# RG-LRU gate products one column tile later, two attention gate tiles moved behind them, and the rotary key's low part on GpSimd, in a two-layer decoder trunk

## The chip, the cores and the metric

The kernel runs on one core of a Trainium2 chip. The time is in microseconds (us) of device time for one execution of the whole program, both layers. The engines are TensorE (PE in the profile, PEld for its weight loads), VectorE (DVE), ScalarE (ACT), GpSimd (POOL) and SyncE (SP), which issues the DMAs. All five run at once, each through its own instructions in a fixed order, and wait for each other on semaphores.

## The reference

A trunk of two layers on x of 1024 tokens and 1024 features, float32. In each layer one combined projection of the normalised input feeds three token mixers; each branch is multiplied by a SiLU gate of the same projection, and the branches go through one output projection into the residual:

```python
h = rmsnorm(x, norm_gain)
proj = h @ w_in
(gq, gk, gv, gb, ga, gz, mq, mkv, mkr, mz, lx, lz) = jnp.split(proj, offsets, axis=-1)
# A: gated DeltaNet (GDN), 4 heads of 128, chunks of 64
o_a = rmsnorm(gated_delta_rule(q, k, v, g, beta), gdn_out_norm) * jax.nn.silu(gz)
# B: latent attention, 8 heads; mkr is the rotary key shared by all heads
k_pe = apply_rope(mkr[:, :, None, :], cos, sin)
o_b = causal_block_attention(qf, kf, vm) * jax.nn.silu(mz)
# C: RG-LRU, 512 channels in 8 blocks of 64
u = causal_dwconv(lx, lru_conv_w) + lru_conv_b
r = jax.nn.sigmoid(u @ w_r + b_r)          # block-diagonal
i = jax.nn.sigmoid(u @ w_i + b_i)
log_a = -8.0 * r * jax.nn.softplus(-a_param)
a = jnp.exp(log_a)
b = jnp.sqrt(-jnp.expm1(2.0 * log_a)) * (i * u)
o_c = associative_scan(h_t = a_t * h_(t-1) + b_t) * jax.nn.silu(lz)
return x + jnp.concatenate([o_a, o_b, o_c], axis=-1) @ w_out
```

## The kernel before

Activations stand with features on the 128 partitions and the 1024 tokens along the free axis. **Products in three passes.** Every float32 operand of a matmul is split into a high part (a copy rounded to the format TensorE takes) and a low remainder, and `mm3` adds high x high, low x high and high x low, so three matmuls per product. `split` makes the two parts of an activation (ACT copies, DVE or POOL subtracts), `load_w` those of a weight: DMA to `wst`, `whi` by a DVE cast (by ACT for the small gate weights), `wlo` by a POOL subtraction.

**Column tiles.** `in_tile` makes one tile of the combined projection, 128 columns by 1024 tokens: 8 input blocks x 2 halves x 3 passes = 48 matmuls into a PSUM tile `pbig`. There are two such PSUM tiles, so a tile can begin only when the tile two before it has been read out; the weight buffers are two deep as well. After a tile stands what reads it: `conv` (one ACT pass and three DVE passes) for a convolved column tile, or a SiLU (`silu2`: ACT tanh, one DVE pass `z`) in `gate_tile`, whose result goes to memory (`mzd` for the attention gates mz, `gzd` for the GDN gates gz).

**What sets the order.** The program is traced in one order, and a scheduler then places instructions on their engines by priority, in the order in which their inputs can be ready. The matmuls of `in_tile` are traced inside a region whose priority is lowered by 20000: they are filler that goes wherever other work leaves TensorE free; the conversions and convolutions beside them are raised by as much. Two consecutive matmuls of a tile may so have other work between them.

**The stages of a layer.** `phase_a` runs GDN for two pairs of heads. While one pair goes through its steps (tokens, `pre`, the inverse of the chunk matrices on DVE in 30 small steps, `prep`, `scan`, and a normalisation with gating, whose last passes are `gzh` on DVE), a generator yields filler tiles; `FILL` says how many at which step. The fillers of pair 0 are gz0, gz1, some mz tiles and the q, k, v tiles of pair 1; those of pair 1 are the latent tiles of the attention, gz2, gz3 and the other mz tiles. There are 8 mz tiles: `MZ1` of them go with pair 1, `MZ2` after the RG-LRU, and the rest, 8 - MZ1 - MZ2, with pair 0. Then comes `lru`: four lx tiles with convolution and gate products; for all four then exponent, square root and scan; four lz tiles with the gating (`of`, split into `oh`, `ol`); the late mz tiles; and the loads of GDN's output (`oaf`, split into `oah`, `oal`). `out_proj` with w_o1 follows: 16 half tiles of 24 matmuls each over `oa` and `oh`, into the banks `pspr`, which DVE adds to the residual `xt`. Meanwhile `split_latents` prepares the attention, among it the rotary key (`rope`, then `kp` and `kl`). Phase C is the attention, with the rest of the output projection in it.

In `lru` the u tiles (`lu`, four of them) lie in buffers of a pool that opens when GDN's pool closes; `uh` and `ul` have one buffer each. The gate products of one tile are 12 matmuls into the two banks `pssc`: two gates x two halves x three passes.

## Time and profile before

| | us |
|---|---|
| median of three runs | 2173.77 (2172.88 to 2176.52) |
| the profiled execution | 2180.79 |
| its span, first to last instruction | 2179.0 |
| TensorE busy | 2060.8 (95%), 10380 matmuls |
| VectorE busy | 1320.7 (61%) |
| ScalarE busy | 882.8 (41%) |
| GpSimd busy | 731.1 (34%) |
| mean granted TensorE clock | 0.986 |

A row of the timeline gives the start in us from the beginning of the span, the duration, the engine, the line of the kernel, the operation, output<-input with shapes, and in brackets how long the engine stood idle before it and what it waited for. In layer 0 the RG-LRU runs from about 495 to 610 us and the first output projection from there to about 700; in layer 1 they begin at about 1570 and 1670 us. A matmul of 512 columns is shown 0.39 us long, but the next starts 0.227 us after it: the end is modelled.

### The profile page before, as it was taken

The numbers are of one execution on the slowest core, as the hardware profiler recorded it, in microseconds if no ns is written. First come the engines' busy times: TensorE is split into PE (matmuls) and PEld (weight loads), VectorE is DVE, ScalarE is ACT, GpSimd is POOL, SyncE is SP. The second block draws the span as 40 slices with busy tenths as digits, with TensorE's granted clock in tenths as the row PEclk, the third lists the DMA queues.
The fourth block names the chain that finished last, engine by engine and source line by source line (L and its number), as shares of the span: only waits on it lengthen the run. The fifth ranks groups of instructions, "written<-read, shape, count | busy, mean of one in ns | idle before, by whom it ended". The sixth has DMA issues, their size and how long they took to land. (4 is left out here: it accounts for less than half of the span.)

```text
span 2179.0 us, 28798 instructions
## 1 busy us (share of the span) xinstructions
PE 2060.8 (95%) x10380; PEld 1683.7 (77%) x10380; DVE 1320.7 (61%) x2498; ACT 882.8 (41%) x1790; POOL 731.1 (34%) x784
## 2 busy tenths in 40 slices
PE   6999999999989999999889999999998999999997
PEld 3788887787767788888668888788876877878874
DVE  6546556555852777776665476474468237676766
ACT  5251244135720554553542413531375125444534
POOL 3222333234452333332242313333336323232322
PEclk9999999999999999999999999999999999999999
DMA  4223212323253115335421331134223520335172
GB/s 142 80 79 97 78 58 93 95 80 102 67 176 131 31 38 185 103 122 181 144 82 49 93 102 46 62 107 131 69 68 113 172 96 27 114 108 170 60 232 97
DMA packets 135102, 222.07 MB, mean 102 GB/s; under 512 B 37808, under 2 KB 60336, under 8 KB 134960
## 3 DMA queue, kind: packets, MB, share of 16 engines
q1 hardware_dynamic: 134960, 220.24, 31.1%
q8 instruction: 82, 1.34, 0.3%
q14 instruction: 60, 0.49, 0.1%
HBM read 147.31 MB, written 72.88 MB: 101 GB/s over the span
## 5 line engine op out<-in xcount | busy, mean ns | idle before, releaser
L112 POOL TENSOR_TENSOR wlo<-wst,whi 128x1024 fp32r<-128x1024 f32 (+3 forms) x196 | 316.1, 1613 | 834.5 <-DVE whi L111 308.9
L121 PE MATMUL pbig<-h,whi 128*128 128x512 f32 x1216 | 484.4, 399 | 8.9 <-ACT h L127 5.9
L123 PE MATMUL pbig<-h,wlo 128*128 128x512 f32 x1216 | 485.1, 399 | 4.0 <-POOL wlo L112 4.0
L122 PE MATMUL pbig<-h,whi 128*128 128x512 f32 x1216 | 484.7, 399 | 3.4 <-DVE h L128 1.6
L121 PEld LDWEIGHTS pbig<-h,whi 128*128 128x128 f32 x1216 | 231.3, 190 | 55.1 <-ACT h L127 6.7
L122 PEld LDWEIGHTS pbig<-h,whi 128*128 128x128 f32 x1216 | 230.8, 190 | 52.4 <-POOL h L128 4.5
L123 PEld LDWEIGHTS pbig<-h,wlo 128*128 128x128 f32 x1216 | 231.0, 190 | 48.5 <-POOL wlo L112 5.3
L86 ACT ACTIVATE P<-pS,mx,scq 128x512 f32<-128x512 f32 (+1 forms) x192 | 128.2, 671 | 155.2 <-DVE mx L89 84.2
L111 DVE CAST whi<-wst 128x1024 fp32r<-128x1024 f32 x92 | 78.2, 850 | 154.7 <-PE pbig L122 122.5
L95 POOL TENSOR_SCALAR P<-P,mx 128x128 f32<-128x128 f32 (+6 forms) x112 | 81.2, 725 | 217.3 <-DVE mx L773 130.1
L109 ACT CAST whi<-wst 128x256 fp32r<-128x256 f32 (+2 forms) x104 | 46.2, 446 | 203.3 <-DMA wst<-in_w_uq 106.2
L127 ACT CAST pth<-pstp 128x512 fp32r<-128x512 f32 x192 | 91.2, 479 | 76.0 <-PE pstp L802 76.0
L762 DVE TENSOR_REDUCE mx<-pS 128x1 f32<-128x512 f32 (+1 forms) x192 | 106.4, 554 | 17.1 <-PE pS L756 11.1
L128 DVE TENSOR_TENSOR ptl<-pstp,pth 128x512 fp32r<-128x512 f32 x192 | 104.7, 551 | 14.7 <-ACT pth L127 13.9
L86 ACT ACT_TABLE_LOAD x81 | 103.9, 1283 | 2.7 <-PEq L1176 0.7
L802 PE MATMUL pstp<-con,P 128*128 128x128 f32 x576 | 97.8, 275 | 5.7 <-DVE P L777 5.0
L92 DVE TENSOR_TENSOR xt<-pspj,xt 128x512 f32<-128x512 f32 x96 | 66.2, 689 | 53.4 <-PE pspj L123 24.6
L121 PE MATMUL pspj<-lh,whi 128*128 128x512 f32 x208 | 85.5, 411 | 6.7 <-DVE k L128 6.0
L802 PEld LDWEIGHTS pstp<-con,P 128*128 128x128 f32 x576 | 71.7, 141 | 25.2 <-DVE P L777 7.3
L813 PE MATMUL pspo<-pth,vh 128*128 128x512 f32 x192 | 79.0, 412 | 6.6 <-ACT pth L127 6.6
L123 PE MATMUL pspj<-lh,wlo 128*128 128x512 f32 x208 | 82.7, 398 | 0.4 <-POOL wlo L112 0.4
L122 PE MATMUL pspj<-ll,whi 128*128 128x512 f32 x208 | 83.0, 399 | 0.0
(270 smaller groups left out, 4566.1 us busy)
## 6 DMA issues: line engine op xcount, KB each, us to landing
wst<-in_w_in SPq DMA_DIRECT2D x76, 512.0 KB, 3.6
x<-xt SPq DMA_DIRECT2D x128, 256.0 KB, 3.4
xt<-x SPq DMA_DIRECT2D x112, 256.0 KB, 3.5
mzd<-z SPq DMA_DIRECT2D x16, 512.0 KB, 3.5
wst<-in_w_o SPq DMA_DIRECT2D x16, 512.0 KB, 3.6
mz<-mzd SPq DMA_DIRECT2D x32, 256.0 KB, 2.9
wst<-in_w_o SPq DMA_DIRECT2D x64, 128.0 KB, 2.1
xk<-x SPq DMA_DIRECT2D x32, 256.0 KB, 4.2
```

The lines of the kernel that those rows point to most:

```text
L86: self.nc.scalar.activation(out, in_, func, **kw)
L95: self.nc.gpsimd.tensor_scalar(out, a, s, 1.0, ALU.mult, ALU.mult)
L111: nc.vector.tensor_copy(hi[:, :n], st[:, :n])
L112: (eng or nc.gpsimd).tensor_tensor(lo[:, :n], st[:, :n], hi[:, :n].bitcast(F32), ALU.subtract)
L121: nc.tensor.matmul(out, ah, bh, start=(j == 0), stop=False)
L122: nc.tensor.matmul(out, ah, bl, start=False, stop=False)
L123: nc.tensor.matmul(out, al, bh, start=False, stop=(j == n - 1))
L127: self.nc.scalar.copy(hi, x)
L128: (eng or self.nc.vector).tensor_tensor(lo, x, hi.bitcast(F32), ALU.subtract)
L762: nc.vector.tensor_reduce(mx[:, j : j + 1], S[j], AX.X, ALU.max, negate=True)
L802: nc.tensor.transpose(tp[:, qi * 128 : qi * 128 + 128], P[qi][:, kb * 128 : kb * 128 + 128], self.ident)
L813: nc.tensor.matmul(po[:, w], vh[:, vs], th[:, w], start=(j == 0), stop=False)
```

## The change

Three things. First, the gate products of tile m are a generator now: its first part (split of u, the gate's weight) is traced behind lx tile m, its second part (the products) behind lx tile m+1. The first matmul of each tile's gates is also pinned, in the order of TensorE's instructions, behind every one traced before it. Second, one filler mz tile fewer is made in each GDN pair (MZ1 from 4 to 3, MZ2 from 0 to 2), and these two are made in `lru`: one before the gate products of tile 3, the other behind the lz tiles. Third, the subtraction that gives `kl`, 64x512 twice per layer, moves from DVE to GpSimd.

```diff
--- before.py
+++ after.py
@@ -113,12 +113,14 @@
         return (hi[:, :n].rearrange("p (k c) -> p k c", k=nk),
                 lo[:, :n].rearrange("p (k c) -> p k c", k=nk))
 
-    def mm3(self, out, pairs):
+    def mm3(self, out, pairs, behind=False):
 
         nc = self.nc
         n = len(pairs)
         for j, (ah, al, bh, bl) in enumerate(pairs):
-            nc.tensor.matmul(out, ah, bh, start=(j == 0), stop=False)
+            first = nc.tensor.matmul(out, ah, bh, start=(j == 0), stop=False)
+            if behind and j == 0:
+                self.tc.keep_in_program_order(first)
             nc.tensor.matmul(out, ah, bl, start=False, stop=False)
             nc.tensor.matmul(out, al, bh, start=False, stop=(j == n - 1))
 
@@ -524,17 +526,16 @@
     def lru(self, l):
         nc, pa, par = self.nc, self.pa, self.par
         st, res = [], []
-        for m in range(4):
-            p = self.in_tile(l, MT_LX + m)
-            u = pa.tile([128, T], F32, name="u", tag="lu", bufs=4)
-            with self.prio(-self.LOW):
-                self.conv(u, p, par[:, C_LCONV + 4 * m : C_LCONV + 4 * m + 4], bias=par[:, C_LCB + m : C_LCB + m + 1])
+
+        def gate_products(m, u):
+
             uh = pa.tile([128, T], F32R, name="uh", tag="uh", bufs=1)
             ul = pa.tile([128, T], F32R, name="ul", tag="ul", bufs=1)
             for n, eng in ((0, nc.gpsimd), (1, nc.vector)):
                 s = slice(n * H2, (n + 1) * H2)
                 self.split(uh[:, s], ul[:, s], u[:, s], eng)
             hi, lo = self.load_w(self.i["w_lru"][l, m], 2, 128, pool=pa)
+            yield
             gt = []
             for k in range(2):
                 t = pa.tile([128, T], F32, name="lg", tag=("lr", "li")[k], bufs=4)
@@ -542,7 +543,7 @@
                 for n in range(2):
                     s = slice(n * H2, (n + 1) * H2)
                     pg = self.bank("sc")
-                    self.mm3(pg, [(hi[:, k], lo[:, k], uh[:, s], ul[:, s])])
+                    self.mm3(pg, [(hi[:, k], lo[:, k], uh[:, s], ul[:, s])], behind=(k == 0 and n == 0))
                     self.act(t[:, s], pg, AF.Sigmoid, bias=par[:, cb : cb + 1])
                 gt.append(t)
             r, ii = gt
@@ -551,6 +552,26 @@
             th = ii
             self.act(th, r, AF.Tanh, scale=self.c8[:, m : m + 1])
             st.append((u, r, th))
+
+        late = iter(range(8 - self.MZ2, 8))
+
+        def late_gate():
+            for h in itertools.islice(late, 1):
+                self.gate_tile(l, MT_MZ + h, self.mzd[h], pa.tile([128, T], F32, name="z", tag="lt", bufs=2))
+
+        prev = None
+        for m in range(4):
+            p = self.in_tile(l, MT_LX + m)
+            u = pa.tile([128, T], F32, name="u", tag="lu", bufs=4)
+            with self.prio(-self.LOW):
+                self.conv(u, p, par[:, C_LCONV + 4 * m : C_LCONV + 4 * m + 4], bias=par[:, C_LCB + m : C_LCB + m + 1])
+            for _ in prev or ():
+                pass
+            prev = gate_products(m, u)
+            next(prev)
+        late_gate()
+        for _ in prev:
+            pass
         for m in range(4):
             u, a, th = st[m]
             self.act(a, a, AF.Exp, scale=self.c8n[:, m : m + 1])
@@ -577,8 +598,7 @@
                         self.silu2(z[:, s], p[:, s])
                 self.gate_split(st[m][2][:, s], 0.5, z[:, s], oh[:, s], ol[:, s], nc.vector if m == 3 else nc.gpsimd)
             res.append((oh, ol))
-        for h in range(8 - self.MZ2, 8):
-            self.gate_tile(l, MT_MZ + h, self.mzd[h], pa.tile([128, T], F32, name="z", tag="lt", bufs=2))
+        late_gate()
         oa = []
         for h in range(4):
             f = pa.tile([128, T], F32, name="oaf", tag="li", bufs=4)
@@ -655,7 +675,7 @@
             kr = self.rope(kx[0:64, s], 64, s)
             nc.scalar.copy(kp[0:64, s], kr)
             nc.scalar.copy(kp[64:128, s], kr)
-            self.tt(kl[0:64, s], kr, kp[0:64, s].bitcast(F32), ALU.subtract)
+            nc.gpsimd.tensor_tensor(kl[0:64, s], kr, kp[0:64, s].bitcast(F32), ALU.subtract)
 
             nc.scalar.copy(kl[64:128, s], kl[0:64, s].bitcast(F32))
         self.kp, self.kl = kp, kl
@@ -1002,8 +1022,8 @@
             self.gdn_norm(pr, Q)
             go(99)
 
-    MZ1 = 4
-    MZ2 = 0
+    MZ1 = 3
+    MZ2 = 2
     FILL = ((1, 1, 2, 0, 1), (1, 0, 3, 0, 2))
 
     LAG = 0.1
```

What this does to the instruction order, at three places of layer 0 (layer 1 has the same shapes). Names in it: u, uh, ul are the RG-LRU's convolved tile and its two parts, gzh GDN's gating, pbig a column tile's PSUM, h the normalised input; a number tells buffers apart.

The handover from GDN to RG-LRU, on DVE, before:

```order
L111 CAST whi_4146<-wst_4144 128x1024
L89 SCALAR_TENSOR_TENSOR gzh_3939<-pspr_3934,onh_346,gzh_3939 128x512
L944 TENSOR_SCALAR onh_9697<-par_9291 128x1
L89 SCALAR_TENSOR_TENSOR u_4007<-pbig_3958,par_185,u_4007 128x1023
L89 SCALAR_TENSOR_TENSOR u_4007<-pbig_3958,par_185,u_4007 128x1022
L89 SCALAR_TENSOR_TENSOR u_4007<-pbig_3958,par_185,u_4007 128x1021
L111 CAST whi_4242<-wst_4240 128x1024
L128 TENSOR_TENSOR ul_4013<-u_4007,uh_4012 128x512
L89 SCALAR_TENSOR_TENSOR u_4103<-pbig_4054,par_185,u_4103 128x1023
```

and now:

```order
L111 CAST whi_4100<-wst_4098 128x1024
L89 SCALAR_TENSOR_TENSOR gzh_3821<-pspr_3816,onh_346,gzh_3821 128x512
L964 TENSOR_SCALAR onh_9697<-par_9291 128x1
L89 SCALAR_TENSOR_TENSOR u_3889<-pbig_3840,par_185,u_3889 128x1023
L89 SCALAR_TENSOR_TENSOR u_3961<-pbig_3912,par_185,u_3961 128x1023
L89 SCALAR_TENSOR_TENSOR u_3889<-pbig_3840,par_185,u_3889 128x1022
L89 SCALAR_TENSOR_TENSOR u_3961<-pbig_3912,par_185,u_3961 128x1022
L89 SCALAR_TENSOR_TENSOR u_3889<-pbig_3840,par_185,u_3889 128x1021
L89 SCALAR_TENSOR_TENSOR u_3961<-pbig_3912,par_185,u_3961 128x1021
L130 TENSOR_TENSOR ul_3895<-u_3889,uh_3894 128x512
L92 TENSOR_TENSOR u_3889<-u_3889,lg_3977 128x1024
```

Before, the three passes of tile 0's convolution stood together and those of tile 1 behind the low part of tile 0; now the passes of the two tiles alternate, and the low part of tile 0 stands behind all six. The cast ahead of the last gzh is that of lx tile 3 now, and was that of lx tile 2.

The same place on TensorE, before: the end of lx tile 1 and the gate products of tile 0, 47 matmuls behind the end of lx tile 0 (L122 and L123 are the second and third pass of a product):

```order
L123 MATMUL pbig_4054<-h_107,wlo_4051 128x512
L121 MATMUL pbig_4054<-h_108,whi_4050 128x512
L122 MATMUL pbig_4054<-h_116,whi_4050 128x512
L121 MATMUL pssc_4025<-uh_4012,whi_4020 128x512
L123 MATMUL pbig_4054<-h_108,wlo_4051 128x512
L122 MATMUL pssc_4025<-ul_4013,whi_4020 128x512
L123 MATMUL pssc_4025<-uh_4012,wlo_4021 128x512
L121 MATMUL pssc_4030<-uh_4012,whi_4020 128x512
L121 MATMUL pbig_4150<-h_101,whi_4146 128x512
```

and now, from the last two matmuls of lx tile 1 on (L124 and L125 are the second and third pass now):

```order
L124 MATMUL pbig_3912<-h_116,whi_3908 128x512
L125 MATMUL pbig_3912<-h_108,wlo_3909 128x512
L121 MATMUL pbig_4008<-h_101,whi_4004 128x512
L121 MATMUL pssc_3967<-uh_3894,whi_3902 128x512
L124 MATMUL pssc_3967<-ul_3895,whi_3902 128x512
L125 MATMUL pssc_3967<-uh_3894,wlo_3903 128x512
L121 MATMUL pssc_3972<-uh_3894,whi_3902 128x512
L124 MATMUL pbig_4008<-h_109,whi_4004 128x512
```

Before, the gate products of tile 0 stood at the end of lx tile 1; now they stand behind the first matmul of lx tile 2. The gate products of tile 1 stand behind the end of lx tile 2, and so on.

The end of the inverse of pair 1, on DVE (inv and itmp are its steps, z a gate's pass), before:

```order
L92 TENSOR_TENSOR itmp_2731<-inv_2730 64x58
L92 TENSOR_TENSOR inv_2730<-inv_2730,itmp_2731 64x2x29
L92 TENSOR_TENSOR itmp_2731<-inv_2730 64x30
L92 TENSOR_TENSOR inv_2730<-inv_2730,itmp_2731 64x30
L393 COPY inv_2730<-inv_2730 64x32x32
L111 CAST whi_3473<-wst_3471 128x1024
L89 SCALAR_TENSOR_TENSOR z_3304<-z_3304,pbig_3255 128x1024
```

and now:

```order
L92 TENSOR_TENSOR inv_2671<-inv_2671,itmp_2672 64x5x26
L92 TENSOR_TENSOR itmp_2672<-inv_2671 64x108
L89 SCALAR_TENSOR_TENSOR z_3245<-z_3245,pbig_3196 128x1024
L92 TENSOR_TENSOR inv_2671<-inv_2671,itmp_2672 64x4x27
L92 TENSOR_TENSOR itmp_2672<-inv_2671 64x84
L92 TENSOR_TENSOR inv_2671<-inv_2671,itmp_2672 64x3x28
L92 TENSOR_TENSOR itmp_2672<-inv_2671 64x58
L92 TENSOR_TENSOR inv_2671<-inv_2671,itmp_2672 64x2x29
L92 TENSOR_TENSOR itmp_2672<-inv_2671 64x30
L92 TENSOR_TENSOR inv_2671<-inv_2671,itmp_2672 64x30
L395 COPY inv_2671<-inv_2671 64x32x32
L111 CAST whi_3577<-wst_3575 128x1024
```

The z pass that stood behind the copy at the end of the steps now stands seven steps ahead of that end.

The end of the RG-LRU on GpSimd, before (ol and oal are the low parts of the RG-LRU's and of GDN's output, wlo is lz tile 3's weight):

```order
L112 TENSOR_TENSOR wlo_4571<-wst_4568,whi_4570 128x1024
L128 TENSOR_TENSOR ol_4421<-of_4428,oh_4420 128x512
L128 TENSOR_TENSOR oal_4641<-oaf_4638,oah_4640 128x1024
L128 TENSOR_TENSOR ol_4489<-of_4492,oh_4488 128x512
L128 TENSOR_TENSOR ol_4489<-of_4496,oh_4488 128x512
L128 TENSOR_TENSOR oal_4647<-oaf_4644,oah_4646 128x1024
L112 TENSOR_TENSOR wlo_4665<-wst_4662,whi_4664 128x1024
```

and now:

```order
L112 TENSOR_TENSOR wlo_4512<-wst_4509,whi_4511 128x1024
L130 TENSOR_TENSOR oal_4641<-oaf_4638,oah_4640 128x1024
L130 TENSOR_TENSOR ol_4430<-of_4433,oh_4429 128x512
L130 TENSOR_TENSOR ol_4430<-of_4437,oh_4429 128x512
L130 TENSOR_TENSOR oal_4647<-oaf_4644,oah_4646 128x1024
L130 TENSOR_TENSOR oal_4653<-oaf_4650,oah_4652 128x1024
L112 TENSOR_TENSOR wlo_4583<-wst_4580,whi_4582 128x1024
L130 TENSOR_TENSOR oal_4659<-oaf_4656,oah_4658 128x1024
L130 TENSOR_TENSOR ol_4498<-of_4501,oh_4497 128x512
```

The first wlo of the rows of now is again lz tile 3's; the second, the weight of the second late mz tile, has come in between the third and the fourth oal.

## The prediction

> **What bounds the kernel now.** I read the page first, then the windows around the RG-LRU stage, then TensorE's waits there, then the timeline of the engines that it waits for.
>
> ```profile
> span 2179.0 us, 28798 instructions
> PE 2060.8 (95%) x10380; PEld 1683.7 (77%) x10380; DVE 1320.7 (61%) x2498; ACT 882.8 (41%) x1790; POOL 731.1 (34%) x784
> ```
>
> TensorE is busy for 95% of the span, and the change neither adds nor removes a matmul. So the time can move in two ways only: by what TensorE stands still (2179.0 − 2060.8 = 118 us), and by what it does at the lower clock. The windows (columns: PE, PEld, DVE, ACT, POOL busy, granted clock, DMA share, GB/s) show where layer 0 has such time:
>
> ```profile
> 470.00:520.00 50.00, 49.80 (x252) 39.20 (x251) 22.77 (x47) 17.10 (x38) 17.11 (x22) 1.00 0.32 106
> 560.00:570.00 10.00, 7.59 (x26) 5.50 (x25) 5.48 (x4) 9.20 (x10) 4.05 (x2) 0.83 0.15 52
> 605.00:610.00 5.00, 4.63 (x12) 3.34 (x12) 4.42 (x5) 2.95 (x5) 5.00 (x4) 0.66 0.01 4
> 648.00:655.00 7.00, 6.60 (x22) 5.30 (x23) 0.94 (x2) 0.00 (x0) 2.26 (x1) 0.76 0.57 185
> 1684.00:1688.00 4.00, 4.00 (x12) 3.08 (x11) 2.35 (x4) 0.62 (x1) 0.00 (x0) 0.56 0.89 323
> ```
>
> Where GDN hands over to RG-LRU (470 to 520), TensorE loses nothing: 49.80 of 50 us at clock 1.00. It loses in the gate products (560 to 570) and at the head of the output projection. The list of all of TensorE's waits (us in total, times, longest) has seven rows that fall wholly in these two places of the two layers:
>
> ```profile
> PE pssc L122 <- POOL ul L128: 5.9, 6, 1.6
> PE pssc L121 <- ACT uh L127: 2.6, 2, 1.8
> PE pspr L121 <- DVE xt L92: 4.6, 2, 3.7
> PE pspr L121 <- ACT oh L127: 3.9, 1, 3.9
> PE pspr L122 <- DVE ol L128: 3.0, 2, 1.6
> PE pspr L122 <- POOL oal L128: 2.5, 2, 1.8
> PE pspr L123 <- POOL wlo L112: 1.3, 1, 1.3
> ```
>
> Gate products (the first two rows) 8.5 us, output projection 15.3: together 23.8 us in 16 waits. These the change can reach.
>
> **What it saves.** *Gate products.* Before a gate product stand a convolution (ACT 1.21, three DVE passes 3.9), the half's copy and its remainder:
>
> ```profile
> 506.10 1.21 ACT L86 ACTIVATE u<-pbig,par 128x1024 f32<-128x1024 f32 x1 [11.72 <-PE pbig L123]
> 507.39 3.91 DVE L89 SCALAR_TENSOR_TENSOR u<-pbig,par,u 128x1023 f32<-128x1023 f32 x3
> 513.29 1.13 ACT L127 CAST uh<-u 128x512 fp32r<-128x512 f32 x2
> 514.15 1.30 POOL L128 TENSOR_TENSOR ul<-u,uh 128x512 fp32r<-128x512 f32 x1
> ```
>
> That is 1.2 + 3.9 + 0.6 + 1.3 = 7 us. In the changed order the gates of tiles 1, 2 and 3 stand 39 to 43 filler matmuls behind the tile's end, at 0.227 us each 9 to 10 us and more with the other gates between: the 8.5 us of waits go. *Output projection.* One whole tile (48 matmuls, 10.9 us) more now stands between the last gates and w_o1; the waits there for oh, ol, oal and wlo (3.9 + 3.0 + 2.5 + 1.3 = 10.7) are each shorter than this and go. *Rotary key.* The two waits for xt, 3.7 and 0.9, stand here:
>
> ```profile
> 644.52 1.25 POOL L673 TENSOR_TENSOR rw<-rw 64x512 f32<-64x512 f32 x1
> 646.46 0.68 DVE L92 TENSOR_TENSOR kl<-rw,kp 64x512 fp32r<-64x512 f32 x1 [3.17 <-ACT kp L656]
> 647.67 1.27 DVE L92 TENSOR_TENSOR xt<-pspr,xt 128x512 f32<-128x512 f32 x2
> ```
>
> DVE stood 3.17 us in front of kl, and the xt that frees TensorE's bank stood behind it. With kl on GpSimd, DVE is past it, so 4.6 us go. GpSimd now stands there instead. What is behind it is the next wlo, which it would begin about 1.3 us later than now (a 64x512 operation of GpSimd took 1.25 there); the matmuls of that weight come 24 matmuls, 5.5 us, later, so I cost this at nothing (0 to 1.5 us).
>
> To the 23.8 us add 16 × 0.16 = 2.6, since a matmul is shown 0.39 long but the next may start 0.227 after it, so each wait costs 0.16 more than its idle time. And the clock:
>
> ```profile
> 562.77 0.50 PE L121 MATMUL pssc<-uh,whi 128*128 128x512 f32 x1 [1.79 <-ACT uh L127]
> 564.13 0.50 PE L122 MATMUL pssc<-ul,whi 128*128 128x512 f32 x1 [0.62 <-POOL ul L128]
> ...
> 566.96 0.63 PE L121 MATMUL pbig<-h,whi 128*128 128x512 f32 x1
> 567.38 0.63 PE L122 MATMUL pbig<-h,whi 128*128 128x512 f32 x1
> ```
>
> After these waits matmuls start 0.42 us apart instead of 0.227 for some 3.4 us; 8 of them lose 1.6 us. Four of the windows above show this (clock 0.83, 0.66, 0.76, 0.56), all behind waits that go: 4 × 1.6 = 6.3. Saved in all: 23.8 + 2.6 + 6.3 = **32.7 us**.
>
> The Trainium skill ("TensorE: Matmul & The Clock Gate", Part 1) says the array falls to half rate only after an idle window of about 3.4 us. Here it fell after waits of 1.79 and 0.62 us, so the trace goes further than the rule. By the rule only the waits of 3.7 and 3.9 us would have cost clock, the saving would be 2 × 1.6 = 3.2 us less, and the forecast 2180 us.
>
> **What it costs.** *The handover.* In the changed order tiles lx0 and lx1 are both finished when GDN's normalisation ends, since u's buffers open only then, and DVE has both convolutions to do at once. It alternates them: u0, u1, u0, u1, u0, u1. They stand behind the gzh pass of the last quarter, and that behind a weight cast that waits for lx1's last matmuls. TensorE's next matmul, the first of lx2, needs u0's bank. The same pieces in the profile of before:
>
> ```profile
> 505.67 0.39 PE L123 MATMUL pbig<-h,wlo 128*128 128x512 f32 x1
> 505.94 0.69 DVE L111 CAST whi<-wst 128x1024 fp32r<-128x1024 f32 x1 [1.35 <-PE pbig L122]
> 506.55 0.74 DVE L89 SCALAR_TENSOR_TENSOR gzh<-pspr,onh,gzh 128x512 f32<-128x512 f32 x1
> ```
>
> From the last matmul of the tile (505.67, call it T) to DVE's first convolution pass (507.39) it is 1.7 us. Now u0's third pass is the fifth of the row: T + 1.7 + 5 × 1.30 = T + 8.2. Only then lx2's first matmul runs, and right behind it stand gates 0, which before had lx1's 47 matmuls in front of them: the copy uh0 (0.6) to T + 8.8, then ul0 on GpSimd (1.3 to 1.8) to T + 10.3. TensorE runs two matmuls in that time; it loses 10.3 − 0.2 − 0.5 + about 0.2 for the second half = 9.8 us. The lower end is 8 us (uh0 and ul0 found ready sooner), the upper 12 (ul 1.87 and DVE's half beside it 1.76). The lower clock behind it: 1.6. The transposes before it:
>
> ```profile
> 495.71 5.60 POOL L95 TENSOR_SCALAR at<-at,ms 128x128 f32<-128x128 f32 x16 [1.85 <-DVE ms L92]
> 499.21 1.08 PE L501 MATMUL pspr<-con,at 128*128 128x128 f32 x4
> ```
>
> have 18 filler matmuls in front of them instead of 33, 3.4 us less cover, and GpSimd gives out four scaled blocks per 1.4 us where TensorE takes 1.08. The chain ahead is shorter too, as no gate tile lies in it; I put 1.0 (0 to 3). Sum 9.8 + 1.6 + 1.0 = **12.4 us a layer** (9 to 16), where nothing is lost now.
>
> *The inverse of pair 1.* TensorE arrives there one tile earlier, because one filler tile has gone from each pair; it needs the bank of gz2, whose gating pass now stands inside the long chain of inverse steps on DVE. Now it stands behind the chain:
>
> ```profile
> 374.53 0.69 DVE L111 CAST whi<-wst 128x1024 fp32r<-128x1024 f32 x1 [3.97 <-PE pbig L122]
> 375.62 2.33 DVE L92 TENSOR_TENSOR itmp<-inv 64x84 f32<-64x84 f32 x1
> 403.52 0.24 DVE L92 TENSOR_TENSOR itmp<-inv 64x84 f32<-64x84 f32 x1
> 404.77 0.18 DVE L92 TENSOR_TENSOR inv<-inv,itmp 64x30 f32<-64x30 f32 x1
> 408.01 0.50 PE L121 MATMUL pbig<-h,whi 128*128 128x512 f32 x1 [0.66 <-DVE z L89]
> 409.39 0.50 PE L123 MATMUL pbig<-h,wlo 128*128 128x512 f32 x1 [0.64 <-POOL wlo L112]
> ```
>
> The chain ends at 404.95 and loses the 3.97 us wait for the cast; it also loses one GpSimd operation beside it (each makes two steps last 2.33 instead of 0.24, so 4.2). The pass stands seven steps, 1.7 us, ahead of its end: about 404.95 − 4.0 − 4.2 − 1.7 + 1.2 (its own length) = 396 to 398. TensorE arrives at 394 to 396. I take 3.0 us (0 to 5), and 0.8 for an even chance of the lower clock, less the 1.6 that the two waits above cost now: **2.2 a layer**.
>
> *The last late tile.* Its wlo stands on GpSimd behind two oal, which wait for an oaf load, which waits for DVE's of:
>
> ```profile
> 591.68 1.06 ACT L127 CAST oah<-oaf 128x1024 fp32r<-128x1024 f32 x1 [2.46 <-DMA oaf<-oad]
> 592.82 3.47 POOL L128 TENSOR_TENSOR oal<-oaf,oah 128x1024 fp32r<-128x1024 f32 x1 [0.86 <-ACT oah L127]
> 597.07 2.40 POOL L112 TENSOR_TENSOR wlo<-wst,whi 128x1024 fp32r<-128x1024 f32 x1 [0.78 <-PE pbig L123]
> ```
>
> Two oal (2.85 to 3.5 each) and the wlo (2.4) are 8 to 9.4 us between the load and the third matmul of a tile that covers 10.9; the load itself came 2.46 us late. I take 2.5 us (0 to 5), and 0.7 (0 to 1.5) for lz3, whose bank waits for lz1's pass: **3.2 a layer**.
>
> **Sum.** 2 × (12.4 + 2.2 + 3.2) = 35.6 lost, 32.7 saved: +2.9 us. The profiled run took 2180.79 us, 1.8 more than its span and 7.0 more than the median of the runs; it becomes 2183.7, and the median 2173.77 becomes **2177**. About 0.2%, 4.3 us, is what a measurement of this kernel can tell from no change. By the ends of the handover alone the sum goes from −4 to +10.
>
> **Rivals.** *Only the handover pays* (25%). The inverse chain is short enough and GpSimd early enough that both later stalls are nothing; the waits of 2 × 1.6 on the inverse go too. Then −32.7 + 24.8 − 3.2 = −11: 2163. For it: both prices have 0 as their lower end. Against: two more tiles stand on GpSimd's queue at the place where it is already fullest (605:610 has it busy 5.00 of 5).
>
> *GpSimd becomes the bound at the end of RG-LRU* (23%). If the oaf load lands more than about 2 us later than TensorE's start of lz3, the late tile's wlo costs its upper 5 us plus 1.6 of clock, and the oal behind it come late to w_o1, so that 1.8 + 0.7 us stay: (5 + 1.6 − 2.5) × 2 + 2.5 = +11 over my sum, 2188. For it: oal took 3.47 and 2.85 us there, of 128x1024, when DVE worked beside it. Against: the tile's own 10.9 us.
>
> *Gates and projection go on waiting* (4%). The pinned first product could leave TensorE's order as it was; then the gate waits (8.5) stay and so does the handover without a stall: 2173.8 − 4.6 for xt = 2169, on the edge of what can be told. Against: the instruction order shows the gates moved.
>
> **Chances.** Forecast 48% (half of it within 0.2%, two fifths slower, one tenth faster), the rivals 25% faster, 23% slower and 4% same. Faster 0.25 + 0.05 = 0.30, same 0.24 + 0.04 = 0.28, slower 0.23 + 0.19 = 0.42. The range takes the first rival's 2163 and the second's 2188: 2163 to 2189; the forecast's own is 2170 to 2184.
>
> **What would show it.** Right: in each layer a wait of 7 to 8.5 us before lx2's first matmul, released by DVE's u, then one of 1 to 2 us for ul; DVE's row of six alternating convolution passes right before; no wait for uh or ul of later gates; none of over 1 us for xt in the first output projection. Wrong: less than 5 us lost there, or more than 8 us in waits for wlo and oal between the gates and w_o1. I would be most wrong if the handover's loss were hidden after all, since it is three quarters of what I charge.

## The result, and the profile after: 2.7% slower

The changed kernel takes 2232.87 us (median of 4 runs, 2231.05 to 2235.77), the kernel before, on the same chip, 2175.14 (2172.88 to 2180.05): a ratio of 1.0268, 95% interval 1.0250 to 1.0286. It is slower, by 58 us, where 3 us were forecast; the time lies far above the range, which ended at 2189.

The page of the changed kernel begins with

```profile
span 2229.2 us, 28790 instructions
PE 2077.9 (93%) x10380; PEld 1692.2 (76%) x10380; DVE 1315.5 (59%) x2494; ACT 869.8 (39%) x1780; POOL 732.3 (33%) x788
```

Between the two profiled executions the span grew by 50.2 us (by less than 58, since the profile of before is of its slowest run and that of the changed kernel of its fastest). TensorE's idle time grew from 118 to 151 us and its busy time by 17, with the same 10380 matmuls: that part is lower clock (a mean of 0.977 after 0.986). In the list of TensorE's waits of the changed kernel (us in total, times, longest), these rows have come in or are what is left of those shown before:

```profile
PE pbig L121 <- ACT sq L86: 19.3, 2, 9.6
PE pbig L125 <- POOL wlo L112: 10.2, 5, 3.4
...
PE pbig L121 <- ACT whi L109: 7.5, 1, 7.5
PE pbig L121 <- DVE u L89: 7.3, 1, 7.3
...
PE pspr L121 <- DVE xt L92: 6.2, 4, 2.3
...
PE pbig L121 <- DVE lz L89: 5.2, 3, 1.8
...
PE pbig L121 <- DVE y L89: 4.4, 2, 2.2
PE pspr L503 <- POOL at L95: 4.3, 4, 1.1
...
PE pssc L124 <- POOL ul L130: 1.3, 2, 0.7
```

The waits of the gate products, 8.5 us before, are 1.3; those for oh, ol and oal are gone; those for xt have grown from 4.6 to 6.2. The wait at the handover is there, once a layer, 7.5 and 7.3 us (the first is put down to ACT's weight cast, which ended at the same time as DVE's pass). But the largest wait, 9.6 us in each layer, is one that the prediction did not have.

To put everything on one scale, I took for each matmul the time from its start to the next one's, less the lower quartile of that time among matmuls of its shape, and added this up between marks that both kernels have. It holds idle time, pacing and lower clock together:

```
time that TensorE loses, us (layer 0 / layer 1)   before        changed       difference
start of the layer to pair 0's normalisation      45.7 /  88.4  50.6 /  91.0   +4.9 /  +2.6
(layer 1's figure holds the attention of layer 0)
pair 0's normalisation to pair 1's                25.3 /  25.0  39.7 /  39.6  +14.4 / +14.6
pair 1's normalisation to the first gate product   3.6 /   3.6  11.7 /  11.6   +8.1 /  +8.0
first gate product to the first of w_o1            7.8 /   5.5  12.5 /  14.5   +4.7 /  +9.0
w_o1 to phase C                                   11.3 /  11.8   5.9 /   5.0   -5.4 /  -6.8
phase C of layer 1                                57.4          54.2           -3.2
sum                                              285.3         336.4          +51.1
```

So more than half of the loss, 29 us, arises inside GDN's second pair, ahead of the handover, where the prediction had put it.

**Where the 9.6 us come from.** The rows of the changed kernel around it (DVE, ACT, then TensorE; start, duration, and in brackets the idle time before with what ended it):

```profile
372.87 3.25 DVE L92 TENSOR_TENSOR rb<-rb,sq 128x1024 f32<-128x1024 f32 x1
376.15 2.48 DVE L89 SCALAR_TENSOR_TENSOR mkvf<-mkvf,par,rb 128x1024 f32<-128x1024 f32 x2
...
376.15 1.11 ACT L86 ACTIVATE mqf<-pbig,par 128x1024 f32<-128x1024 f32 x1 [7.03 <-DVE rb L92]
378.66 1.02 ACT L86 ACTIVATE sq<-pbig 128x1024 f32<-128x1024 f32 x1 [1.40 <-DVE mkvf L89]
...
379.74 0.80 PE L121 MATMUL pbig<-h,whi 128*128 128x512 f32 x1 [9.63 <-ACT sq L86]
```

TensorE has finished two of the three query latent tiles and needs the first one's bank for the third. ACT reads that bank twice, into mqf and into sq, and both go into the four buffers that the key-value latents still fill until DVE has normalised them (rb, mkvf). The same two reads in the kernel before:

```profile
365.15 1.12 ACT L86 ACTIVATE mqf<-pbig,par 128x1024 f32<-128x1024 f32 x1 [4.60 <-DVE rb L92]
370.23 1.03 ACT L86 ACTIVATE sq<-pbig 128x1024 f32<-128x1024 f32 x1 [3.96 <-DVE mkvf L89]
```

They waited there too, but the bank was free at 371.3, and TensorE came to the third tile only when the second ended, at 374.5: 3.2 us to spare. Now it comes at 370.1 and the bank is free at 379.7. TensorE is 4.4 us earlier since it had one tile (10.9 us) less to do, though it has lost part of that on the way; the chain is late by 8.4; and 4.4 + 8.4 less the 3.2 to spare are the 9.6. Why the chain is late, is to be seen on ACT at the end of pair 0 (changed kernel):

```profile
310.31 1.06 ACT L86 ACTIVATE th<-wq 128x1024 f32<-128x1024 f32 x1 [0.62 <-DVE wq L89]
311.27 0.99 ACT L643 COPY mkvf<-pbig 128x1024 f32<-128x1024 f32 x1
313.46 1.03 ACT L86 ACTIVATE sq<-pbig 128x1024 f32<-128x1024 f32 x1 [1.20 <-PE pspr L295]
...
315.86 0.31 ACT L86 ACTIVATE ms<-ms,ep 128x16 f32<-128x16 f32 x1
...
317.67 0.22 ACT L86 ACTIVATE ms<-ms 128x16 f32<-128x16 f32 x1
```

ms is the root with which pair 0's normalisation begins; its two operations start at 315.9 and 317.7. Before, they started at 304.4 and 307.0:

```profile
304.39 0.31 ACT L86 ACTIVATE ms<-ms,ep 128x16 f32<-128x16 f32 x1
```

With a tile fewer ahead of them, the last q tile of pair 1 and the first latent tile come while pair 0's last quarter is still running, and their convolution and their readings, which have the higher priority, stand in front of its chain on DVE and ACT.

**The handover** went much as forecast: six passes in a row on DVE, the gate's weight arriving in the same microsecond, and the gates behind (changed kernel, DVE, ACT, POOL, TensorE):

```profile
515.70 7.22 DVE L89 SCALAR_TENSOR_TENSOR u<-pbig,par,u 128x1023 f32<-128x1023 f32 x6
...
521.32 0.40 ACT L109 CAST whi<-wst 128x256 fp32r<-128x256 f32 x1 [5.66 <-DMA wst<-in_w_lru]
...
521.81 0.74 POOL L112 TENSOR_TENSOR wlo<-wst,whi 128x256 fp32r<-128x256 f32 x1 [4.29 <-ACT whi L109]
522.51 1.27 POOL L130 TENSOR_TENSOR ul<-u,uh 128x512 fp32r<-128x512 f32 x1
...
521.87 0.77 PE L121 MATMUL pbig<-h,whi 128*128 128x512 f32 x1 [7.45 <-ACT whi L109]
522.49 0.79 PE L121 MATMUL pssc<-uh,whi 128*128 128x512 f32 x1
523.84 0.80 PE L124 MATMUL pssc<-ul,whi 128*128 128x512 f32 x1 [0.56 <-POOL ul L130]
```

**The last late tile** waits for its low weight behind two oal, as forecast, but longer (POOL, TensorE):

```profile
613.07 4.73 POOL L130 TENSOR_TENSOR oal<-oaf,oah 128x1024 fp32r<-128x1024 f32 x2 [1.29 <-ACT oah L129]
617.76 2.80 POOL L112 TENSOR_TENSOR wlo<-wst,whi 128x1024 fp32r<-128x1024 f32 x1
...
620.61 0.79 PE L125 MATMUL pbig<-h,wlo 128*128 128x512 f32 x1 [3.41 <-POOL wlo L112]
```

The windows of the changed kernel (PE, PEld, DVE, ACT, POOL busy, granted clock, DMA share, GB/s) show the clock that goes with these three places:

```profile
365.00:390.00 25.00, 15.37 (x55) 11.79 (x55) 18.73 (x30) 8.01 (x8) 4.97 (x2) 0.80 0.35 116
500.00:535.00 35.00, 25.66 (x97) 18.17 (x96) 15.55 (x18) 15.87 (x24) 12.55 (x21) 0.85 0.33 108
600.00:635.00 35.00, 29.43 (x120) 22.96 (x119) 26.18 (x18) 9.85 (x14) 26.46 (x11) 0.95 0.35 120
```

### The profile page after: what moved, and what is told of

Read it like the earlier page. It is cut to its first block, busy times and chain, and to the rows that moved or that the text cites. A ratio compares the mean times of both kernels' runs of the same rounds, so it can differ in the third digit from the quotient of the medians.

```text
span 2229.2 us, 28790 instructions
## 1 busy us (share of the span) xinstructions
PE 2077.9 (93%) x10380; PEld 1692.2 (76%) x10380; DVE 1315.5 (59%) x2494; ACT 869.8 (39%) x1780; POOL 732.3 (33%) x788
## 4 chain that ended last, share of the span: by engine, by line
PE 51%; DVE 6%; ACT 4%; DMA 4%; issue 2%; POOL 2%; SPq 0%; DVEq 0%; ACTq 0%; POOLq 0%
PE pbig L125 5%; PE pbig L124 5%; PE pbig L121 5%; PE pspj L121 4%; PE pspj L124 4%; PE pspj L125 4%; PE pstp L822 2%; PE pspr L121 2%; PE pspr L124 2%; PE pspr L125 2%; PE pspo L835 2%; DMA x<-xt 1%; PE pspo L833 1%; PE pspo L834 1%; PE pS L772 1%
## 5 line engine op out<-in xcount | busy, mean ns | idle before, releaser
L121 PE MATMUL pbig<-h,whi 128*128 128x512 f32 x1216 | 491.6, 405 | 51.8 <-ACT sq L86 19.3
L125 PE MATMUL pbig<-h,wlo 128*128 128x512 f32 x1216 | 489.3, 402 | 10.2 <-POOL wlo L112 10.2
L124 PE MATMUL pbig<-h,whi 128*128 128x512 f32 x1216 | 490.9, 404 | 3.1 <-POOL h L130 1.6
L121 PEld LDWEIGHTS pbig<-h,whi 128*128 128x128 f32 x1216 | 234.4, 193 | 103.6 <-ACT sq L86 20.1
L125 PEld LDWEIGHTS pbig<-h,wlo 128*128 128x128 f32 x1216 | 233.9, 192 | 55.9 <-POOL wlo L112 12.3
L124 PEld LDWEIGHTS pbig<-h,whi 128*128 128x128 f32 x1216 | 234.1, 192 | 52.4 <-DVE h L130 4.3
L125 PE MATMUL pspj<-lh,wlo 128*128 128x512 f32 x208 | 82.2, 395 | 0.3 <-POOL wlo L112 0.3
L124 PE MATMUL pspj<-ll,whi 128*128 128x512 f32 x208 | 82.3, 396 | 0.0
```

The lines of the kernel that those rows point to most:

```text
L121: first = nc.tensor.matmul(out, ah, bh, start=(j == 0), stop=False)
L124: nc.tensor.matmul(out, ah, bl, start=False, stop=False)
L125: nc.tensor.matmul(out, al, bh, start=False, stop=(j == n - 1))
```

## The experiments

Ratios are to the kernel before, measured beside each run, with 95% intervals.

**The parts one by one.** Two theories stood against each other: that the tiles taken out of the GDN pairs cause the loss (A), or the later and pinned gate products (B).

The change with the filler count undone:

```diff
-    MZ1 = 3
-    MZ2 = 2
+    MZ1 = 4
+    MZ2 = 0
```

> The change with its filler count undone (MZ1 = 4, MZ2 = 0): gate products one tile later and pinned, kl on GpSimd, no gate tile moved. Theory A, the loss comes from the filler tiles taken out of the GDN pairs, which makes TensorE reach every later stage one or two tiles early: none of the three stalls of the changed kernel (9.6 us before the inverse, 7.4 us at the handover, 3.4 us at the late tile) is left, and the kernel is faster than before: the waits of gates 1 and 2 (about 2 us a layer) and for xt (4.6 us and one spell of the lower clock, 1.6) go, those of gates 3, which have only some 10 filler matmuls behind lx3, and those at the head of the output projection stay. 2164 us, between 2156 and 2172. Theory B, the later and pinned gate products make the handover stall: it is still there, 7 us or more a layer, and the time is 2185 or more.

Measured: 0.9975 (0.9962 to 0.9988). No stall at the handover, none before the inverse. B falls. But the gain is half of the 10 us that I expected.

The kernel before with the filler count alone (the same four lines the other way round):

> The kernel before with nothing but the filler count changed (MZ1 = 3, MZ2 = 2, both late gate tiles at the end of the RG-LRU). Theory A: the stalls before the inverse (about 9.6 us and the lower clock behind it), at the handover (about 7 to 10) and in pair 0 (2 to 3) are all there in both layers, and nothing is saved at the gates or for xt: 2235 us, between 2222 and 2250. Theory B: little happens without the delay, under 2190.

Measured: 1.0308 (1.0285 to 1.0331), 67 us. All the stalls are there, with the same lengths (9.6 before the inverse, 7.5 and 7.3 at the handover). So the filler count alone loses at least as much as the whole change does (the two intervals just touch).

The kernel before with kl alone on GpSimd, and with the gate products alone:

```diff
-            self.tt(kl[0:64, s], kr, kp[0:64, s].bitcast(F32), ALU.subtract)
+            nc.gpsimd.tensor_tensor(kl[0:64, s], kr, kp[0:64, s].bitcast(F32), ALU.subtract)
```

> The kernel before with nothing but kl moved to GpSimd. By the prediction the waits for xt (3.7 and 0.9 us, and 1.6 of lower clock) go and nothing else: 2168 us, between 2166 and 2172. The rival: the wait for xt only changes its place, since in the changed kernel 6.2 us of such waits were left, behind the split of the latents and casts: 2174, within 2.

> The kernel before with the later and pinned gate products alone. The run with this and kl was as fast as the one with kl alone, so it is worth nothing: within 0.2% of the kernel before. The prediction's price for the waits of gates 1 to 3, with the lower clock: 0.3% faster or more.

Measured: kl 0.9974 (0.9961 to 0.9986); the gate products 1.0012 (1.0001 to 1.0024). kl is worth 0.26%, as priced (4.6 us of waits and a spell of lower clock), and is all that the first run gained. Its wait for xt fell from 4.6 to 1.5 us:

```profile
PE pspr L121 <- DVE xt L92: 1.5, 1, 1.5
```

The later gate products do what was forecast of them and gain nothing. By the marks above, the time lost between gates and w_o1 fell from 7.8 and 5.5 to 3.8 and 3.8 us, 5.7 in all; in w_o1 it went from 11.3 and 11.8 to 13.6 and 10.4, so 0.9 came back there. The spans of the two profiles differ by the rest, 5 us, but the timed runs show none of the gain. Their clock tells more: the median of the granted clock is 0.983 in the ten runs of this kernel and 0.987 in the thirteen of the kernel before beside them. Over 2175 us that is 8.7 us of TensorE's time, an estimate (0.004 × 2175), and so more than the idle time that went. Why the clock is lower is not settled.

**Which tile.** One late tile instead of two:

```diff
-    MZ1 = 3
-    MZ2 = 2
+    MZ1 = 4
+    MZ2 = 1
```

> The change with one late gate tile instead of two (MZ1 = 4, MZ2 = 1): pair 0 has 3 filler gate tiles, pair 1 has 4 as before, the late tile stands before gates 3. Theory A: TensorE is one tile ahead through pair 1, so the stall before the inverse (about 10 us and the lower clock, 12 a layer) and that of pair 0 (3) are there, but the convolutions of tiles 0 and 1 are not alternated, so the handover loses less than 3; gates 3 have cover. 30 lost, 25 saved: 2180 us, between 2168 and 2194. If the stall before the inverse does not come from pair 0's missing tile: about 2150.

Measured: 1.0192 (1.0166 to 1.0219), 42 us. The 9.6 us stall is there; the convolutions do not alternate and nothing stands still at the handover. The 25 us that I counted as saved were not saved, though: in layer 0, waits of 3.9 us for w_o1's wlo and 3.8 for oh came up at the head of w_o1.

To take the end of the RG-LRU out of the question, the tile from pair 0 was made at the end of pair 1's filler (on the kernel with kl on GpSimd), and then, instead, as the first of pair 1's filler:

```diff
-    MZ1 = 4
+    MZ1 = 5
```

```diff
         def fill1():
+            yield from itertools.islice(mz, 1)
             yield from self.lat_kv(l)
```

> The kernel before with kl on GpSimd and one gate tile taken out of pair 0 and made at the end of pair 1's filler (MZ1 = 5, MZ2 = 0); the RG-LRU and all behind it have the tiles they had. Theory A, TensorE's being one tile early in pair 1 is the loss: 5 us a layer up to the end of pair 0 and 14 in pair 1, as in the two runs with a tile less in pair 0; with kl alone 2172, so 2210 us, between 2198 and 2218. Rival: the loss of those runs came from the late tile at the RG-LRU's end; then 2180 or less.

> The same, but the gate tile taken from pair 0 is the first of pair 1's filler, in front of the latent tiles, so that these come where they came before. Theory A: the 9.6 us stall before the inverse is gone and only pair 0's part stays: 2180 us, between 2174 and 2188. Rival: what is missing in pair 0 costs, wherever the tile goes: 2205 or more.

Measured: 1.0159 (1.0123 to 1.0194) and 1.0029 (1.0012 to 1.0046), where kl alone is 0.9974. One tile later by two stages, in a layer that has the same tiles and the same RG-LRU, costs 1.9%; put in front of the latents it costs 0.55%. In the second the stall before the inverse is gone altogether. In the first it is as it was:

```profile
379.27 0.79 PE L121 MATMUL pbig<-h,whi 128*128 128x512 f32 x1 [9.62 <-ACT sq L86]
```

The tile from pair 1 alone (on the kernel with kl on GpSimd again):

```diff
-    MZ1 = 4
-    MZ2 = 0
+    MZ1 = 3
+    MZ2 = 1
```

> The kernel before with kl on GpSimd and one gate tile taken from pair 1 alone and made at the end of the RG-LRU (MZ1 = 3, MZ2 = 1). If the losses of the two missing tiles add up: the run with both lost 3.1% and pair 0's share was 1.9%, so pair 1's is 1.2%: 2199 us, between 2190 and 2207, with no stall before the inverse and a stall of 7 us or so at the handover. Rival: the handover stalls only where TensorE is two tiles early: 2185 or less.

Measured: 1.0127 (1.0108 to 1.0146). The two tiles' losses nearly add up: 1.85% for pair 0's (1.0159 against 0.9974) and 1.53% for pair 1's make 3.4%, against 3.1% for both at once (the filler count alone). One tile is enough for the stall at the handover:

```profile
512.91 0.77 PE L121 MATMUL pbig<-h,whi 128*128 128x512 f32 x1 [6.67 <-DVE u L89]
```

**Why pair 0's tile costs more than its own time.** The first run of the pair above (tile at the end of pair 1), with pair 0's last two scan quarters and its normalisation at a higher priority than the fillers' readings:

```diff
-                self.gdn_scan(pr, Q, q)
+                with self.prio(-2 * self.LOW if pr == 0 and q > 1 else 0):
+                    self.gdn_scan(pr, Q, q)
                 go(n[4])
-            self.gdn_norm(pr, Q)
+            with self.prio(-2 * self.LOW if pr == 0 else 0):
+                self.gdn_norm(pr, Q)
```

> The run with one gate tile taken from pair 0 and made at the end of pair 1's filler (2215), with nothing changed but the priority of pair 0's last two scan quarters and its normalisation, which now go ahead of the last q tile's convolution and of the first latent tile's readings on DVE and ACT. Theory G: the missing tile costs twice, since these operations come one tile early and stand in front of pair 0's chain on DVE and ACT (its end 10 us later), and since TensorE has one tile less to do while pair 1's chain runs. With the chain in front about half of the 43 us over the run with kl alone comes back: 2200 us, between 2192 and 2208. Rival: only the tile's own time is missing: 2213 or more.

Measured: 1.0081 (1.0064 to 1.0097). Two fifths of the loss come back (0.78 of 1.85%), and the stall is what the remaining cause should leave: 10.9 us of the missing tile less the 3.2 that were to spare is 7.7.

```profile
370.62 0.79 PE L121 MATMUL pbig<-h,whi 128*128 128x512 f32 x1 [7.62 <-ACT sq L86]
```

The same edit in the changed kernel, and in the kernel with kl alone:

> The changed kernel with pair 0's last two scan quarters and its normalisation put ahead of the last q tile's convolution and the first latent tile's readings. With one tile missing this gave back 0.8%. If the same delay is in the changed kernel, as its stall of 9.6 us before the inverse says, that stall falls to 7.6, the 2.2 us stall of pair 0 goes, and 20 us in all come back: 2213 us, between 2206 and 2222. If the second missing tile takes the gain (TensorE reaches the handover earlier and waits longer there): 2228 or more.

> The kernel before with kl on GpSimd and the same order of pair 0's chain, no gate tile moved. In the run with kl alone pair 0 has neither of the two stalls (2.2 and 9.6 us), so there is little to give back: 2172 us, between 2168 and 2177, no faster than kl alone. If the chain is late there as well, 2165 or less.

Measured: 1.0177 (1.0155 to 1.0198) and 1.0021 (1.0008 to 1.0034). In the changed kernel 0.9% comes back, 20 us, so pair 0's late chain is about a third of its loss. Where no tile is missing the same order costs 0.5%: it is no improvement of its own.

**What sets the length of the stall.** The changed kernel without the refinement of the key-value latents' reciprocal root:

```diff
-        r = self.rms_bcast(self.c4, [acc], T, 256, "pr", fine=True)
+        r = self.rms_bcast(self.c4, [acc], T, 256, "pr")
```

> The changed kernel without the refinement step of the reciprocal root in the norm of the key-value latents (four DVE operations and two reads of the sums; this leaves out part of the computation). These operations took 2.5 + 0.7 + 3.3 us and more of DVE right before the two mkvf passes behind which ACT reads the first query latent out of its PSUM tile. Theory C, that chain sets the stall before the inverse: 9.6 becomes about 3 us in each layer, and 13 us in all go: 2220 us, between 2213 and 2226. Rival D, the prediction's: TensorE waits for the gating pass inside the inverse: the stall stays, 2233.

Measured: 1.0331 (1.0299 to 1.0364), slower still. (This kernel leaves out part of the computation.) The stall did fall, from 9.6 to 4.5 us, so the normalisation does set it and not the gating pass inside the inverse. But the time saved there was lost again further on:

```profile
375.83 0.79 PE L121 MATMUL pbig<-h,whi 128*128 128x512 f32 x1 [4.52 <-ACT sq L86]
...
530.14 0.76 PE L121 MATMUL pbig<-h,whi 128*128 128x512 f32 x1 [14.59 <-DVE u L89]
```

None of it was left at the handover. The first transposes of pair 1's normalisation stand at 508.9 us, in the changed kernel at 504.5; TensorE came to the handover at 515.6, there at 514.4; and DVE's first convolution pass began at 524.0, there at 515.7. DVE's last gating pass in front of it waited for a load:

```profile
515.37 0.69 DVE L111 CAST whi<-wst 128x1024 fp32r<-128x1024 f32 x1 [2.89 <-PE pbig L124]
516.71 0.75 DVE L89 SCALAR_TENSOR_TENSOR gzh<-pspr,onh,gzh 128x512 f32<-128x512 f32 x1 [0.65 <-DMA gzh<-gzd]
523.11 0.75 DVE L89 SCALAR_TENSOR_TENSOR gzh<-pspr,onh,gzh 128x512 f32<-128x512 f32 x1 [5.65 <-DMA gzh<-gzd]
```

Why pair 1's chain and that load came later was not followed up.

**The handover.** The convolution of tile 1 put behind that of tile 0 in the changed kernel, by an order on DVE alone (an excerpt; `behind` is set for tile 1 only):

```diff
+            if behind and d == 1:
+                self.tc.add_manual_dep(
+                    op.ins, self.conv_end.name,
...
+        self.conv_end = op.ins
```

> The changed kernel with the first convolution pass of lx tile 1 put behind the last of tile 0 on DVE, so that the six passes no longer alternate. Theory E, the alternating order sets the stall at the handover: tile 0 is ready two passes, 2.4 us, sooner, and the stall of 7.4 us falls to 5: 2228 us, between 2224 and 2231. Rival F: the gate weight, whose load lands at the same time (ACT's cast waits for the load until 521.3, and the low part of u stands behind the weight's low part on GpSimd), sets it as well; then TensorE's first matmul comes sooner, the gates do not, and the time is 2232 or 2233.

Measured: 1.0263 (1.0231 to 1.0296), against 1.0268 for the changed kernel. The wait is in two parts now, and they add up to the same:

```profile
520.27 0.77 PE L121 MATMUL pbig<-h,whi 128*128 128x512 f32 x1 [5.33 <-DVE u L155]
522.94 0.79 PE L121 MATMUL pssc<-uh,whi 128*128 128x512 f32 x1 [1.90 <-ACT uh L129]
524.45 0.80 PE L124 MATMUL pssc<-ul,whi 128*128 128x512 f32 x1 [0.72 <-POOL ul L130]
```

F holds: the load of the gate's weight ends as late as the alternating passes, and the wait changes its name.

**The end of the RG-LRU.** Both late tiles in front of gates 3; and, in the changed kernel again, GDN's heads 0 and 2 split by DVE:

```diff
         late_gate()
+        late_gate()
         for _ in prev:
...
-        late_gate()
         oa = []
```

```diff
-            self.split(oh, ol, f, nc.gpsimd)
+            self.split(oh, ol, f, nc.gpsimd if h % 2 else nc.vector)
```

> The changed kernel with both late gate tiles in front of gates 3, so that no weight of a late tile stands behind the low parts of GDN's output on GpSimd. Theory H, that place in GpSimd's queue costs 3.4 us and the lower clock behind it: the 8 us a layer lost between the lz tiles and w_o1 go, some 4 of the waits at the head of w_o1 come back: 2224 us, between 2214 and 2230. Rival: GpSimd is behind there in any case and the wait only moves into w_o1: 2232 or more.

> The changed kernel with the low parts of GDN's heads 0 and 2 made by DVE instead of GpSimd, so that one instead of three of them stands ahead of the late tile's weight. Theory I, GpSimd's queue sets the 3.4 us wait for that weight: the wait goes, with the lower clock behind it, 5 us a layer or nearly, and DVE's two operations of 1.2 us cost less: 2224 us, between 2219 and 2230. Rival: DVE and GpSimd are both full there, DVE's own passes come later and TensorE waits for lz and of instead: 2231 or more.

Measured: 1.0307 (1.0292 to 1.0323) and 1.0272 (1.0246 to 1.0297). Neither is faster. In the first the wait for a late tile's weight is gone and three others stand at the head of w_o1:

```profile
633.13 0.79 PE L125 MATMUL pspr<-oah,wlo 128*128 128x512 f32 x1 [3.80 <-POOL wlo L112]
...
643.70 0.79 PE L121 MATMUL pspr<-oh,whi 128*128 128x512 f32 x1 [4.43 <-ACT oh L129]
...
645.82 0.80 PE L124 MATMUL pspr<-ol,whi 128*128 128x512 f32 x1 [1.32 <-DVE ol L130]
```

In the second the 3.4 us for wlo are down to 0.4, and xt takes their place:

```profile
617.98 0.50 PE L125 MATMUL pbig<-h,wlo 128*128 128x512 f32 x1 [0.36 <-POOL wlo L112]
...
651.04 0.80 PE L121 MATMUL pspr<-oah,whi 128*128 128x512 f32 x1 [5.79 <-DVE xt L92]
```

Between the first gate and phase C TensorE loses, in layer 0 and layer 1, 19.1 and 17.3 us in the kernel before, 18.4 and 19.5 in the changed one, 21.6 and 20.3 with both late tiles early, 18.4 and 16.6 with oal on DVE. Moving a tile or a split there mostly changed which result TensorE waits for. The sum is no constant, though: over all the kernels profiled here it lies between about 14 and 24 us a layer. Nor is one of the other engines full: in the 203 us of layer 0 in the changed kernel DVE is busy for 95, GpSimd for 80 and ACT for 76. That GpSimd's queue alone sets it is refuted; what does is not settled.

Of all these, kl alone on GpSimd is the fastest, with the run without moved tiles (0.9975) beside it: 0.9974 of the kernel before, and 2.9% under the changed one.

## Why the prediction was wrong

By its own terms, both layers, us (lost is positive; the last column from the marks above and from the windows and waits inside them):

```
term                                          predicted   measured
gate products, with their clock                  -11.4      -10.6
oh, ol, oal, wlo, xt, with their clock           -21.3      -12.2
handover (wait, clock, transposes)               +24.8      +23.8
pair 0                                              0        +7.5
pair 1 (inverse)                                  +4.4      +29.0
late tile and lz3                                 +6.4      +16.6
attention                                           0        -3.2
sum                                               +2.9      +50.9
```

How the measured loss between gates and w_o1 divides among gate products, handover and late tile is read off single waits and spells of lower clock; each of the three can be off by some 2 us. The attention is a stage that the change does not touch; over all the profiles its loss in layer 1 spreads by 6 us, so its -3.2 says nothing.

**The gate products** were right, in place and size, as far as their waits go; alone they brought no time, where the prediction's price was 0.3% or more. **The handover** was right: six alternating passes, 7.5 us of wait (8 predicted), then ul (0.6 us, 1 to 2 predicted), then the lower clock. In part that was luck: the alternating alone does not set it, since the gate's weight, which the prediction left out, comes no sooner. It is not the seven tenths of the cost that the sum gave it (24.8 of 35.6; the prediction calls it three quarters), but three tenths.

**The step that failed is "the inverse of pair 1".** It said that TensorE arrives there one tile earlier, which is right, and then looked for the first wait in the inverse itself (gz2's gating pass, 0 to 5 us; 2.2 a layer in the sum). The wait is at the stage ahead of it, 9.6 us for the query latents' bank, and there TensorE had 3.2 us to spare where a tile is 10.9; with what follows it, pair 1 loses 14.5 us a layer. I had the row that shows the bank waiting for DVE's normalisation, and did not ask of each bank between GDN's start and the handover how long it had been free when TensorE came. The experiments put the stall there: it goes when the tile is put back in front of the latents, and shrinks when the normalisation is shortened.

**Missing altogether was pair 0.** The prediction took the GDN chains as given and moved TensorE against them. But a filler tile brings its convolution and its readings to DVE and ACT, at a higher priority than the chain: one tile earlier, they fell into pair 0's last quarter and made that chain 8 to 11 us later, which TensorE paid for again in pair 1. With the chain put first, 0.8 and 0.9% came back.

**The late tile** was the right wait in the right place, but too cheap: 2.5 us for wlo and 0.7 for lz were charged, 3.4 and 1.7 (3.5 in layer 1) measured, and a spell of lower clock stands behind them, for which nothing was charged. And 9 us of **what the output projection was to save** were not saved: xt kept 6.2 us of waits, since the latents' split and the casts on DVE now fall into w_o1 at another place. The rival that had GpSimd as the bound at the end of the RG-LRU, 2188, came near for that weight (3.4 us and the lower clock where it had 5 and 1.6), but the waits for oal that it kept are gone, and it, too, had the pairs without a loss.

**kl** was right, alone: 0.26%.

## What to carry to other kernels

Here, filler work taken out of a stage that another engine's chain holds up did not shorten that stage. It left TensorE idle there and was paid for again where it went. So before a filler tile is moved, list for every bank and buffer between the old place and the new one how long it had been free when it was taken, and look for the first that has less to spare than the tile is long; then ask which operations of the other engines come earlier with it, and whose chain they stand in front of. And a wait is not its price: 3.4 us for a weight and 5 of the 9.6 us were removed here, and neither kernel became faster, since TensorE waited at the next place instead.

## What the runs showed of the hardware

One and the same wait, 2.2 us in pair 0 at the y pass, stands 18 times in the profiles of nine of these kernels. In the 6 us behind it the granted clock was 1.00 in five cases and 0.72 in thirteen, with nothing between. The windows of the changed kernel and of the one with the filler count alone, in layer 0:

```profile
307.92:313.92 6.00, 6.00 (x34) 5.15 (x35) 1.83 (x4) 4.15 (x8) 1.27 (x1) 1.00 0.27 87
```

```profile
306.24:312.24 6.00, 6.00 (x24) 4.95 (x24) 1.81 (x4) 3.69 (x7) 1.25 (x1) 0.72 0.29 87
```

The same 6 us hold 34 matmuls or 24. What decides is where the wait falls. In each of the 17 profiles, the spells of the lower clock begin whole multiples of 3.41 us apart, as if on a grid, and each but the last is one to five times 3.41 us long. The 2.2 us began 0.3 to 1.1 us behind a point of that grid in the thirteen cases, so that they lay between two points, and 2.6 to 2.9 us behind one in the five, so that a point cut them. The grid lies otherwise in every run (the first spell began 15.0 us into the span in the kernel before, 16.4 in the changed one, 17.3 with kl alone). So a sum made ahead of the run can price such a wait only by a share (here 0.7 × 1.7 us). The Trainium skill ("TensorE: Matmul & The Clock Gate", Part 1) says that the window in which activity is counted runs freely and does not start with the kernel; the grid agrees with that. Its figure of about 3.4 us of idling does not agree with 2.2.

A 128x1024 subtraction on GpSimd took 2.40 us where it began 0.5 us ahead of an operation of DVE, and 4.23 where it began 0.2 us behind a scan of DVE (two rows of GpSimd and two of DVE, changed kernel):

```profile
584.70 2.40 POOL L112 TENSOR_TENSOR wlo<-wst,whi 128x1024 fp32r<-128x1024 f32 x1 [14.66 <-DVE whi L111]
...
601.34 4.23 POOL L112 TENSOR_TENSOR wlo<-wst,whi 128x1024 fp32r<-128x1024 f32 x1 [2.86 <-issue]
...
585.17 3.00 DVE L92 TENSOR_TENSOR u<-u,lg 128x1024 f32<-128x1024 f32 x1 [0.70 <-ACT lg L86]
...
601.13 2.28 DVE L585 TENSOR_TENSOR_SCAN lg<-lg,u 128x1024 f32<-128x1024 f32 x1
```

The 4.23 are about what was left of the scan, 2.1 us, and then GpSimd's own 2.4. In the first case it was DVE that took longer: 3.00 us, up to 1.1 us behind the end of GpSimd's, where the median of these operations in the kernel before is 1.23. The Trainium skill ("SBUF — State Buffer", Who interferes with whom) says that an operation of DVE with two inputs in SBUF competes with GpSimd's reads for a port that they share, and that of the two engines the one that comes second stands still until the first is done; both pairs of rows agree with it. The late tile's weight was not held up by this: GpSimd stood idle for 1.29 us ahead of the two oal in front of it.
